# Two units' weight casts a half product earlier, one cast kept in order, and a one-column Tanh behind each Sqrt

## The chip, the cores and the metric

The kernel runs on one core of a Trainium2 chip. The metric is the device time of one execution in microseconds (us): before the change the median of three runs is 928.36 us (927.94 to 928.42). The engines are PE (matrix multiplies, with its weight loads PEld), DVE (vector), ACT (scalar: copies, casts and functions), POOL (issues stores here) and SP (issues loads here).

## The reference

One layer of a hybrid decoder, for one new sequence of 1024 tokens and for 8 single decode tokens, model width 1024. One input projection feeds an RG-LRU group and an mLSTM group of four heads:

```
hn = rmsnorm(x, g_norm);  u = hn @ w_in          # 1024 x 7176
xa, za, uq, uk, uv, uo, zb, ui, uf = split(u)
RG-LRU:  xc = causal 4-tap conv of xa
         r, i = sigmoid(block-diagonal gates of xc)      # 16 blocks of 64
         a = exp(-8 r softplus(-lambda))
         u = sqrt(-expm1(2 log a)) * (i * xc);  h_t = a_t h_(t-1) + u_t
mLSTM:   chunks of 128 tokens, running-max stabiliser, C and n carried
merged = [h * silu(za),  headnorm(sigmoid(uo) * h_mlstm) * silu(zb)]
y = rmsnorm(x + merged @ w_out, g_final)
```

The outputs are y for prompt and decode tokens and all recurrent states, in float32. The two big products, with w_in and w_out, are where most matrix work lies.

## The kernel before

**Products.** The columns of w_in are done in 14 units of 512 columns (two blocks of 256, `UNITS`, index u from 0 to 13; in tile names the unit's index is the last part of `raw_4`). A unit is a 2x2 block product done as seven products instead of eight, in the order P1, P2, P5, P6, P7, P3, P4; the number in `wh_3` is the product's place in that order, 0 to 6, so `wh_3` belongs to P6 and `wh_6` to P4. Each float32 factor is split into a rounded part and a rest, so each product needs three matmuls where one would stand: `mm3` at L64 (hi by hi), L65 and L66. In one half product that is 12 matmuls with 512 columns.

**Weight casts.** `prep` makes a product's factors: on ACT the rounded part (L278, `wh`), on DVE the rest (L281, `wl`), for some products with a sum or difference of raw blocks ahead (L272 to L275, L284). It runs two products (`LEAD = 2`) ahead of the product that uses them. `load_raw` (L217 ff.), called from `prep` of P7 and P4, issues the next unit's loads on SP. L1555 sets how far ahead: normally a product's `prep` is written ahead of the whole product; for u in 2 to 7, one that falls due with product n is written behind product n's first half.

**Evacuation.** `evac` takes each half product from PSUM: ACT copies (L321, L328, L331, L346) or DVE adds (L324, L334, L338). There are two PSUM buffers `kv`, three `o` and one each of `s`, `qp`, `tr`.

**Background work.** Between half products `pop_bg` issues one step each of queues of other work. In units 1 to 11 the main one is the RG-LRU, 16 halves (8 groups of 128 channels by 2 halves of 512 tokens) of eight steps: `conv1`, `conv2`, an empty one, `gate_a`, `gate_b`, `decay`, `scan`, `outs`. The gates are matmuls at L874 and, on ACT, a Tanh at L828 (`rg`, then `ig`; a Tanh with scaled input is the sigmoid); `gate_b`'s matmul writes the single `s` buffer that `gate_a`'s two Tanhs read. `decay` ends with a Sqrt on ACT (L896); `scan` is L900 to L902 on DVE; `outs` multiplies by the gate z (L906) and splits the result: `split` (L70 cast `rmh` on ACT, L71 rest `rml` on DVE), then two stores on POOL to `d_rm`. A decode step (`dec_unit`, L234) adds 32-row matmuls at each unit's P1 boundary, and the decode of the mLSTM adds matmuls at L1036 and ACT work at L1017.

**Order.** A scheduler orders each engine's instructions; an instruction that is pinned (`keep_in_program_order`) stays in the order written against the other pinned ones. From u = 2 on every `wh` cast is pinned. ACT holds one set of functions at a time; an `ACT_TABLE_LOAD` precedes an instruction whose function is not in the set held. Sqrt is in one set here, Tanh and Exp in another; copies and casts need no load.

Of the kernel before, what the change touches and what calls it, by code (L numbers as in the profile page):

```python
# [9 lines left out]
F32 = mybir.dt.float32  # L10
F32R = mybir.dt.float32r
BF16 = mybir.dt.bfloat16
AF = mybir.ActivationFunctionType
ALU = mybir.AluOpType
# [30 lines left out]
NWS, NSTG, LEAD = 6, 7, 2  # L45
# [4 lines left out]
def hymba_kernel(  # L50
# [7 lines left out]
    V, A, G, TE = nc.vector, nc.scalar, nc.gpsimd, nc.tensor  # L58
# [9 lines left out]
    def split(hi, lo, src):  # L68

        A.copy(hi, src)  # L70
        V.tensor_tensor(lo, src, hi.bitcast(F32), op=ALU.subtract)  # L71

    pin = tc.keep_in_program_order
# [7 lines left out]
    def ps(tag, shape):  # L81
        return psp.tile(shape, F32, tag=tag, name=f"ps_{tag}", bufs=NBUF.get(tag, 1))

    def const(shape, name, dt=F32):
        return cpool.tile(shape, dt, tag=name, name=name)
# [14 lines left out]
    def sg(shape, name, dt=F32):  # L100

        return stg.tile(shape, dt, tag="stg", name=name)
# [4 lines left out]
    def dconst(shape, name):  # L107

        return dpool.tile(shape, F32, tag=name, name=name)
# [4 lines left out]
    ones = dconst([P, P], "ones")  # L114
# [262 lines left out]
    warm = const([P, 1], "warm")  # L377
# [389 lines left out]
    def pop_bg(n=1, rg=1, dc=1):  # L767
        run_late()
        for q, m in ((bg, n), (rgq, rg), (dcq, dc)):
            for _ in range(m):  # L770
                if q:
                    q.popleft()()
# [19 lines left out]
    def rg_load(n, both=False):  # L792

        if n >= len(halves) or halves[n][0] not in rst["stored"]:
            return
        j, b = halves[n]
        if ("x", n) not in rst:
            xs = fpr["p"].tile([P, 3 + HT], F32, tag="xs", name="xs", bufs=2)
            if b == 0:
                V.memset(xs[:, 0:3], 0.0)  # L800
                ld(xs[:, 3:3 + HT], d_x[j][:, 0:HT])
            else:
                ld(xs, d_x[j][:, HT - 3:T])
            rst["x", n] = xs
        if both and ("z", n) not in rst:
            rst["z", n] = zs = fpr["p"].tile([P, HT], F32, tag="zsr", name="zsr")
            ld(zs, d_y[j][:, b * HT:(b + 1) * HT])
# [17 lines left out]
    def gate_out(rg, ig, pg, j, n):  # L825

        for m, t in enumerate((rg, ig)):
            A.activation(t[LOHI[n]], pg[LOHI[m]], AF.Tanh, scale=0.5, bias=hb[LOHI[m], j, n:n + 1])  # L828

    def rg_gw(j):  # L830
        if j < KC:
            graw = fpr["graw"][j % 2]
            for n, src in enumerate((w_rgate, w_igate)):
                for s in LOHI:
                    ld(graw[s, :, n * 64:n * 64 + 64], src[0, 2 * j:2 * j + 2].rearrange("t c d -> c t d"))

    def rg_half(j, b):
        fp = fpr["p"]
        pc = lambda r, n=1: PT[:, j, r:r + n]
        st = {}  # L840

        n = 2 * j + b

        def conv1():
            rg_load(n, True)
            xs = st["xs"] = rst["x", n]
            rg_load(n + 1)
            if b == 0:
                rg_gw(j + 1)
                ghi = fp.tile([P, 2, P], F32R, tag="ghi", name="ghi")  # L850
                glo = fp.tile([P, 2, P], F32R, tag="glo", name="glo")
                split(ghi, glo, fpr["graw"][j % 2])
                rst["g", j] = ghi, glo
            st["xc"] = xc = fp.tile([P, HT], F32, tag="xc", name="xc")
            V.tensor_scalar(xc, xs[:, 3:3 + HT], pc(R_CW + 3), pc(R_CB), op0=ALU.mult, op1=ALU.add)
            for t in (2, 1):
                V.scalar_tensor_tensor(xc, xs[:, t:t + HT], pc(R_CW + t), xc, op0=ALU.mult, op1=ALU.add)

        def conv2():
            xs, xc = st["xs"], st["xc"]  # L860
            V.scalar_tensor_tensor(xc, xs[:, 0:HT], pc(R_CW), xc, op0=ALU.mult, op1=ALU.add)
            st["xx"] = [fp.tile([P, HT], F32R, tag=t, name=t) for t in ("xh", "xl")]
            for n, s in enumerate(LOHI):
                x = st["xx"][n]
                A.copy(x[s], xc[s])
                V.tensor_tensor(x[LOHI[1 - n]], xc[s], x[s].bitcast(F32), op=ALU.subtract)
            if b == 1:
                V.tensor_copy(OC[:, j, 1:4], xs[:, HT:HT + 3])

        def gate(n):  # L870

            pg = ps("s", [P, 512])
            for k, w in enumerate(rst["g", j]):
                TE.matmul(pg, w[:, n, :], st["xx"][n], start=k == 0, stop=k == 1)  # L874
            return pg

        def gate_a():
            rg_load(n + 1)
            pg = gate(0)
            st["rg"], st["ig"] = (fp.tile([P, HT], F32, tag=t, name=m) for m, t in (("rg", "rg"), ("ig", "xh")))  # L880
            gate_out(st["rg"], st["ig"], pg, j, 0)

        def gate_b():
            pg = gate(1)
            gate_out(st["rg"], st["ig"], pg, j, 1)
            st["na"] = fp.tile([P, HT], F32, tag="xl", name="na")
            A.activation(st["na"], st["rg"], AF.Tanh, scale=sp2[:, j:j + 1], bias=sp2[:, j:j + 1])
            A.activation(st["rg"], st["rg"], AF.Exp, scale=sp4n[:, j:j + 1], bias=sp4n[:, j:j + 1])
            V.scalar_tensor_tensor(st["ig"], st["ig"], 1.0, st["xc"], op0=ALU.add, op1=ALU.mult)

        def decay():
            rg, na = st["rg"], st["na"]
            V.scalar_tensor_tensor(na, rg, 1.0, na, op0=ALU.add, op1=ALU.mult)
            V.tensor_scalar(rg, na, -1.0, 1.0, op0=ALU.mult, op1=ALU.add)
            V.scalar_tensor_tensor(na, na, 2.0, na, op0=ALU.subtract, op1=ALU.mult)
            A.activation(na, na, AF.Sqrt, scale=-0.25)  # L896

        def scan():
            rg, ig, na = st["rg"], st["ig"], st["na"]
            V.tensor_tensor(ig, ig, na, op=ALU.mult)  # L900
            V.tensor_tensor_scan(na, rg, ig, 0.0 if b == 0 else OC[:, j, 0:1], op0=ALU.mult, op1=ALU.add)
            V.tensor_copy(OC[:, j, 0:1], na[:, HT - 1:HT])  # L902

        def outs():
            na, zs = st["na"], rst["z", n]
            V.scalar_tensor_tensor(na, na, 0.5, zs, op0=ALU.mult, op1=ALU.mult)  # L906
            mh, ml = sg([P, HT], "rmh", F32R), sg([P, HT], "rml", F32R)
            split(mh, ml, na)
            stq(d_rm[0, j, :, b * HT:(b + 1) * HT], mh.bitcast(F32))
            stq(d_rm[1, j, :, b * HT:(b + 1) * HT], ml.bitcast(F32))  # L910
        return [conv1, conv2, lambda: None, gate_a, gate_b, decay, scan, outs]
# [622 lines left out]
    def preps(n):  # L1534
        for what, f in (("dec", prep_dec), ("prep", prep)):
            while what in n and state[what] < min(n[what], len(seq)):
                f(*seq[state[what]])
                state[what] += 1
# [13 lines left out]
    state["prep"] = state["dec"] = LEAD  # L1552
    part = 0
    for n, (u, q) in enumerate(seq):
        lead = {"dec": n + 1 + LEAD, "prep": n + (LEAD if u in range(2, 8) else 1 + LEAD)}  # L1555
        preps(lead)
        for _ in product(u, q):
            pop_bg(2 if u == last_u else 1, 1, part % DEC[1 if u >= DEC[0] else 2] == 1)
            preps({"prep": n + 1 + LEAD})
            part += 1  # L1560
            if u == last_u:
                wo_due((part - 1) % 14)
        if q == 6:
            for kind, j in units[u]:
                if kind == "x":
                    rg_unit(j)
            for half in range(2):
                if u == (unit_of["v", 2 * half + 1] | 1):
                    bg.append(lambda half=half: dec_rows(half))
            for h in range(NH):  # L1570
                if done_h[h] | 1 == u:
                    bg.append(lambda h=h: dcq.extend(decode_steps(h)))
            if u == last_u - 1:
                dgen = decode_outputs()

                def step():
                    next(dgen, None)
                    run_late()
                state["out"] = [step] * 5 + [m_open2]
        if not state["m"] and u > max(done_h) and not (bg or rgq or dcq or late):  # L1580
            m_start()
        if u == last_u and q == 0:
            if not state["m"]:
                while bg or rgq or dcq or late:
                    pop_bg()
                m_start()
            bg.extend(state["out"])
# [113 lines left out]
```

## Time and profile before

| what | value |
|---|---|
| median of three runs | 928.36 us |
| profiled execution, its own time | 926.71 us |
| its span, first to last instruction | 925.0 us |
| granted PE clock, mean | 0.999 |
| PE, PEld busy | 99%, 82% of the span |
| DVE, ACT, POOL busy | 77%, 62%, 17% |
| loads of a function set on ACT, by line | 16 at L896 (Sqrt), 12 at L828, the rest elsewhere |

A matmul's shown duration overlaps its neighbours': matmuls of 512 columns are shown 0.39 us long but start every 0.23 us. So PE's share of busy time says little; what counts is the time from one matmul's start to the next. In the answers shown, each row gives the start, the duration, the engine, the line, the operation, the tile written and those read, and in brackets idle time with what ended it.

### The profile page before, as it was taken

How to read it: one execution, taken by the hardware profiler on the slowest of the kernel's cores; microseconds unless marked ns; L12 is line 12 of the kernel's file. 1: busy time of each engine (PE TensorE's matmuls, PEld its weight loads, DVE VectorE, ACT ScalarE, POOL GpSimd, SP SyncE). 2: the span in 40 equal slices, each digit the busy share in tenths (PEclk: the TensorE clock that was granted, in tenths of full speed). 3: DMA queues.
4: the chain of work that ended last, by engine and by line, in shares of the span. 5: the costliest groups of instructions: out<-in, count | busy, mean ns of one | idle time of the engine just before them, and what ended most of it. 6: DMA issues, size and time to landing. Idle time of an engine off the chain costs nothing.

```text
span 925.0 us, 15327 instructions
## 1 busy us (share of the span) xinstructions
PE 912.6 (99%) x5349; PEld 760.2 (82%) x5349; DVE 708.2 (77%) x1465; ACT 574.0 (62%) x1032; POOL 154.6 (17%) x290
## 2 busy tenths in 40 slices
PE   9999999999999999999999999999999999999997
PEld 8897686878778987777789898876787888888886
DVE  6765986799788878989788866687856777667665
ACT  6753456768587767678577773447646566556552
POOL 1420111011212222222112312010201000000110
PEclk9999999999999999999999999999999999999999
DMA  7342364343656465657636553544963565465431
GB/s 242 107 133 75 116 202 160 119 160 114 207 183 237 157 217 193 208 166 251 202 128 219 181 171 129 171 145 172 346 183 121 162 186 155 115 188 155 125 84 57
DMA packets 131330, 153.69 MB, mean 166 GB/s; under 512 B 15674, under 2 KB 110018, under 8 KB 131246
## 3 DMA queue, kind: packets, MB, share of 16 engines
q1 hardware_dynamic: 113382, 96.58, 34.7%
q0 software_dynamic: 17728, 55.87, 16.5%
q8 instruction: 42, 0.69, 0.3%
q14 instruction: 34, 0.28, 0.1%
q10 hardware_dynamic: 144, 0.26, 0.1%
HBM read 101.10 MB, written 51.65 MB: 165 GB/s over the span
## 4 chain that ended last, share of the span: by engine, by line
PE 87%; DVE 5%; ACT 4%; DMA 1%; issue 1%; POOL 0%; SPq 0%; DVEq 0%; ACTq 0%; POOLq 0%
PE ps_o L64 13%; PE ps_o L66 13%; PE ps_o L65 13%; PE ps_kv L64 10%; PE ps_kv L66 10%; PE ps_kv L65 10%; PE ps_o L534 3%; PE ps_tr L234 3%; PE ps_s L1204 2%; PE ps_s L874 2%; PE ps_qp L64 1%; PE ps_tr L1345 1%; PE ps_qp L65 1%; PE ps_qp L66 1%; PE ps_qp L1036 1%
## 5 line engine op out<-in xcount | busy, mean ns | idle before, releaser
L281 DVE TENSOR_TENSOR wl<-raw,wh 128x1024 fp32r<-128x1024 f32 x91 | 111.0, 1220 | 43.0 <-ACT wh L278 28.4
L64 PE MATMUL ps_kv<-cb_hi,wh 128*128 128x512 f32 x320 | 127.1, 397 | 0.5 <-ACT s L331 0.5
L66 PE MATMUL ps_kv<-cb_hi,wl 128*128 128x512 f32 x320 | 125.3, 392 | 1.3 <-DVE wl L281 1.3
L65 PE MATMUL ps_kv<-cb_lo,wh 128*128 128x512 f32 x320 | 125.3, 392 | 0.0
L278 ACT CAST wh<-raw 128x1024 fp32r<-128x1024 f32 x91 | 95.0, 1045 | 21.2 <-DVE raw L275 6.0
L64 PE MATMUL ps_o<-cb_hi,wh 128*128 128x512 f32 x240 | 94.6, 394 | 0.0
L66 PE MATMUL ps_o<-cb_hi,wl 128*128 128x512 f32 x240 | 93.8, 391 | 0.0
L65 PE MATMUL ps_o<-cb_lo,wh 128*128 128x512 f32 x240 | 93.7, 390 | 0.0
L64 PEld LDWEIGHTS ps_kv<-cb_hi,wh 128*128 128x128 f32 x320 | 60.1, 188 | 19.3 <-issue 4.6
L66 PEld LDWEIGHTS ps_kv<-cb_hi,wl 128*128 128x128 f32 x320 | 60.1, 188 | 15.5 <-DVE wl L281 2.1
L65 PEld LDWEIGHTS ps_kv<-cb_lo,wh 128*128 128x128 f32 x320 | 60.2, 188 | 12.0
L64 PE MATMUL ps_kv<-wh,cb_hi 128*128 128x256 f32 x192 | 55.0, 287 | 0.0
L64 PEld LDWEIGHTS ps_o<-cb_hi,wh 128*128 128x128 f32 x240 | 45.1, 188 | 11.4 <-issue 2.1
L65 PE MATMUL ps_kv<-wl,cb_hi 128*128 128x256 f32 x192 | 54.4, 283 | 0.0
L66 PE MATMUL ps_kv<-wh,cb_lo 128*128 128x256 f32 x192 | 54.3, 283 | 0.0
L66 PEld LDWEIGHTS ps_o<-cb_hi,wl 128*128 128x128 f32 x240 | 45.1, 188 | 9.9 <-DVE wl L281 0.2
L64 PE MATMUL ps_o<-wo,mh 128*128 128x512 f32 (+1 forms) x136 | 53.2, 391 | 0.0
L65 PEld LDWEIGHTS ps_o<-cb_lo,wh 128*128 128x128 f32 x240 | 45.1, 188 | 9.2
L66 PE MATMUL ps_o<-wo,ml 128*128 128x512 f32 (+1 forms) x136 | 51.7, 380 | 0.0
L65 PE MATMUL ps_o<-wo,mh 128*128 128x512 f32 (+1 forms) x136 | 51.6, 380 | 0.0
L64 PE MATMUL ps_o<-wo,rh 128*128 128x512 f32 x120 | 48.3, 403 | 0.0
L66 PE MATMUL ps_o<-wo,rl 128*128 128x512 f32 x120 | 47.3, 394 | 0.0
(509 smaller groups left out, 2450.6 us busy)
## 6 DMA issues: line engine op xcount, KB each, us to landing
raw<-in_w_in_dram SPq DMA_DIRECT2D x56, 512.0 KB
Cb<-in_state_mlstm_C_dram SPq DMA_DIRECT2D x32, 256.0 KB
out_dram<-Cb POOLq DMA_DIRECT2D x32, 256.0 KB, 4.3
qk<-d_qk SPq DMA_DIRECT2D x32, 256.0 KB
oraw<-in_w_out_dram SPq DMA_DIRECT2D x16, 512.0 KB
d_qk<-s POOLq DMA_DIRECT2D x24, 256.0 KB, 3.1
x<-in_x_prompt_dram SPq DMA_DIRECT2D x8, 512.0 KB
d_x<-s POOLq DMA_DIRECT2D x16, 256.0 KB, 2.6
```

Source lines behind the costliest of these rows:

```text
L64: TE.matmul(out, ah, bh, start=first, stop=False, skip_group_check=True)
L65: TE.matmul(out, ah, bl, start=False, stop=False, skip_group_check=True)
L66: TE.matmul(out, al, bh, start=False, stop=last, skip_group_check=True)
L234: TE.matmul(dz_["p"][32 * g:32 * g + 32, :], hnd[:, k, 0:32] if second else hnd[:, k, 8:40], raws[u, k // 4][:, k % 4, :], start=k < 4 and ...
L278: o = A.copy(hi, blk(u, *src[q]))
L281: V.tensor_tensor(lo, blk(u, *src[q]), hi.bitcast(F32), op=ALU.subtract)
L534: TE.matmul(pt, op[k][x], wt, start=(k, x, y) == (0, 0, 0), stop=(k, x, y) == (7, 0, 1), skip_group_check=True)
L874: TE.matmul(pg, w[:, n, :], st["xx"][n], start=k == 0, stop=k == 1)
L1036: TE.matmul(pq[32 * g:32 * g + n, 0:256], qsel[:, kb, 4 * bb:4 * bb + n], ds_["C", h * NB + bb][:, kb, :], start=bb < 2, stop=bb >= NB - 2 ...
L1204: TE.matmul(S, qk[:, 2 + kb, :], qk[:, kb, :], start=kb == 0, stop=kb == 1)
L1345: TE.matmul(dec_o[0][32 * g:32 * g + 32, :], md, oraw[m][:, half * 512:(half + 1) * 512], start=first and m in ms[:2], stop=last and m in ...
```

## The change

Three edits. First, behind each Sqrt of the RG-LRU stands a Tanh of one column into a scratch tile (`warm`), pinned; nothing reads it. Second, in `outs` the cast of `rmh` is pinned; the subtraction is the one that `split` did. Third, L1555's range is cut from u = 2 to 7 to u = 4 to 7, so in the third and fourth units the `prep` that was behind a product's first half is ahead of the product again, with the raw loads that it issues.

```
@@ decay
             A.activation(na, na, AF.Sqrt, scale=-0.25)
+            pin(A.activation(warm, ones[:, 0:1], AF.Tanh))
@@ outs
-            split(mh, ml, na)
+            pin(A.copy(mh, na))
+            V.tensor_tensor(ml, na, mh.bitcast(F32), op=ALU.subtract)
@@ main loop
-        lead = {"dec": n + 1 + LEAD, "prep": n + (LEAD if u in range(2, 8) else 1 + LEAD)}
+        lead = {"dec": n + 1 + LEAD, "prep": n + (LEAD if u in range(4, 8) else 1 + LEAD)}
```

With the change, decay's Tanh is L897, scan L901 to L903, outs L907, the pinned cast L909 and its rest L910.

**ACT at the end of unit u = 2.** Rows in ACT's order; `wh_6` is the factor of the unit's last product, `wh_0` and `wh_1` those of the next unit, and `s` at L331 the two halves of P6. Before:

```order
L331 COPY s_1641<-ps_kv 128x512
L331 COPY s_1663<-ps_kv 128x512
L896 ACT_TABLE_LOAD
L896 ACTIVATE na<-na 128x512
L278 CAST wh_5_1647<-raw_2_1290 128x1024
L865 CAST xh<-xc 64x512
L70 CAST rmh<-na 128x512
L278 CAST wh_6_1689<-raw_2_1290 128x1024
L865 CAST xl<-xc 64x512
L278 CAST wh_0_1741<-raw_3_1602 128x1024
L346 COPY c_1771<-ps_kv 128x512
L828 ACT_TABLE_LOAD
```

With the change:

```order
L278 CAST wh_5_1629<-raw_2_1290 128x1024
L331 COPY s_1645<-ps_kv 128x512
L331 COPY s_1664<-ps_kv 128x512
L278 CAST wh_6_1669<-raw_2_1290 128x1024
L896 ACT_TABLE_LOAD
L896 ACTIVATE na<-na 128x512
L897 ACT_TABLE_LOAD
L897 ACTIVATE warm<-ones 128x1
L865 CAST xh<-xc 64x512
L909 CAST rmh<-na 128x512
L278 CAST wh_0_1720<-raw_3_1580 128x1024
L865 CAST xl<-xc 64x512
```

`wh_5` and `wh_6` now stand ahead of the Sqrt instead of behind it, and the load for Tanh follows the Sqrt instead of standing ahead of the gate.

**PE at the boundary of units u = 2 and 3.** The last matmul of P4, the decode matmuls (L234) and the gate's (L874). Before:

```order
L66 MATMUL ps_kv<-cb_hi_169,wl_6_1690 128x512
L234 MATMUL ps_tr<-raw_3_1602,hnd 32x512
L874 MATMUL ps_s<-xl,ghi 128x512
L874 MATMUL ps_s<-xl,glo 128x512
L234 MATMUL ps_tr<-raw_3_1602,hnd 32x512 x3
L234 MATMUL ps_tr<-raw_3_1693,hnd 32x512 x4
```

With the change:

```order
L66 MATMUL ps_kv<-cb_hi_169,wl_6_1670 128x512
L874 MATMUL ps_s<-xl,ghi 128x512
L874 MATMUL ps_s<-xl,glo 128x512
L234 MATMUL ps_tr<-raw_3_1580,hnd 32x512 x4
L234 MATMUL ps_tr<-raw_3_1673,hnd 32x512 x4
```

The gate's pair no longer stands inside the decode group.

**DVE in unit u = 4, around P6.** `wl_3` is the rest of P6's factor; L901 (before) or L902 (with the change) that writes `na` from `rg` and `ig` is the scan. Before:

```order
L900 TENSOR_TENSOR ig<-ig,na 128x512
L861 SCALAR_TENSOR_TENSOR xc<-xs,PT,xc 128x512
L281 TENSOR_TENSOR wl_3_2267<-raw_4_1958,wh_3_2266 128x1024
L901 SCALAR_TENSOR_TENSOR na<-rg,OC,ig 128x512
L800 MEMSET xs 128x3
L923 COPY dxs<-dxc 64x8
L902 COPY OC<-na 128x1
L906 SCALAR_TENSOR_TENSOR na<-na,zsr 128x512
```

With the change:

```order
L901 TENSOR_TENSOR ig<-ig,na 128x512
L861 SCALAR_TENSOR_TENSOR xc<-xs,PT,xc 128x512
L902 SCALAR_TENSOR_TENSOR na<-rg,OC,ig 128x512
L800 MEMSET xs 128x3
L925 COPY dxs<-dxc 64x8
L903 COPY OC<-na 128x1
L907 SCALAR_TENSOR_TENSOR na<-na,zsr 128x512
L281 TENSOR_TENSOR wl_3_2271<-raw_4_1938,wh_3_2270 128x1024
```

`wl_3` moves behind the scan, two small copies and L907. On ACT the cast `wh_3` that it needs stands right behind the Sqrt before, and behind Sqrt, load and one-column Tanh with the change.

## The prediction

> **What bounds the kernel now.** I read the page first, then the waits of PE from 100 to 600 us, where the projection and the RG-LRU run, then PE's timeline at each gap, then ACT and DVE there. The page:
>
> ```profile
> PE 912.6 (99%) x5349; PEld 760.2 (82%) x5349; DVE 708.2 (77%) x1465; ACT 574.0 (62%) x1032; POOL 154.6 (17%) x290
> ```
>
> PE sets the end. The edits add no matmul, so they can only take gaps between matmuls away or make new ones. The waits view (engine, line waited at, releaser: us, times, longest) names how much there is to take:
>
> ```profile
> PE ps_kv L66 <- DVE wl L281: 1.3, 2, 1.0
> PE ps_s L874 <- ACT ig L828: 0.7, 2, 0.5
> PE ps_kv L64 <- ACT s L331: 0.5, 1, 0.5
> ```
>
> This understates it, since a matmul's shown duration runs into the next one's. I measure from start to start, and take off the 0.23 us at which 512-column matmuls normally follow:
>
> ```profile
> 149.97 0.39 PE L65 MATMUL ps_kv<-cb_lo,wh 128*128 128x512 f32 x1
> 150.68 0.50 PE L66 MATMUL ps_kv<-cb_hi,wl 128*128 128x512 f32 x1 [0.32 <-DVE wl L281]
> ...
> 194.91 0.40 PE L65 MATMUL ps_kv<-cb_lo,wh 128*128 128x512 f32 x1
> 196.26 0.50 PE L66 MATMUL ps_kv<-cb_hi,wl 128*128 128x512 f32 x1 [0.96 <-DVE wl L281]
> 196.60 0.40 PE L64 MATMUL ps_kv<-cb_hi,wh 128*128 128x512 f32 x1
> ...
> 261.62 0.39 PE L64 MATMUL ps_o<-cb_hi,wh 128*128 128x512 f32 x1
> 262.49 0.50 PE L874 MATMUL ps_s<-xl,ghi 128*128 128x512 f32 x1 [0.48 <-ACT ig L828]
> ...
> 313.38 0.28 PE L66 MATMUL ps_kv<-wh,cb_lo 128*128 128x256 f32 x1
> 313.72 0.50 PE L874 MATMUL ps_s<-xl,ghi 128*128 128x512 f32 x1
> ...
> 409.29 0.39 PE L64 MATMUL ps_o<-cb_hi,wh 128*128 128x512 f32 x1
> 410.18 0.50 PE L64 MATMUL ps_kv<-cb_hi,wh 128*128 128x512 f32 x1 [0.50 <-ACT s L331]
> ...
> 418.52 0.39 PE L66 MATMUL ps_o<-cb_hi,wl 128*128 128x512 f32 x1
> 419.16 0.50 PE L874 MATMUL ps_s<-xl,ghi 128*128 128x512 f32 x1 [0.25 <-ACT ig L828]
> ```
>
> So the gaps are 0.48, 1.12, 0.64, 0.22 (0.34 less the 0.12 of a 256-column matmul), 0.66 and 0.41 us. After a wait the next start follows 0.34 us later (196.26 to 196.60) instead of 0.23, so each wait costs 0.11 more. All six together are 4.2 us, 0.45% of the time. Nothing that the edits touch can give much more, except one thing that the waits view does not show, a decode group cut in two at the end of u = 2; beside it a whole one:
>
> ```profile
> 156.39 1.04 PE L234 MATMUL ps_tr<-raw,hnd 128*32 128x512 f32 x2
> 157.37 0.50 PE L874 MATMUL ps_s<-xl,ghi 128*128 128x512 f32 x1
> ...
> 159.88 0.50 PE L64 MATMUL ps_kv<-cb_hi,wh 128*128 128x512 f32 x1
> ...
> 426.54 1.92 PE L234 MATMUL ps_tr<-raw,hnd 128*32 128x512 f32 x16
> 428.40 0.50 PE L64 MATMUL ps_kv<-cb_hi,wh 128*128 128x512 f32 x1
> ```
>
> Cut, the stretch takes 159.88 - 156.39 = 3.49 us with the gate's pair in it. Whole, the group takes 1.86; the pair in a run of full matmuls is 2 x 0.23 = 0.46.
>
> **The change, part by part.** *Earlier casts in u = 2 and 3 (gain).* ACT at the end of u = 2:
>
> ```profile
> 140.89 0.63 ACT L896 ACTIVATE na<-na 128x512 f32<-128x512 f32 x1
> ...
> 148.31 1.05 ACT L278 CAST wh<-raw 128x1024 fp32r<-128x1024 f32 x1
> ...
> 153.89 1.28 ACT L828 ACT_TABLE_LOAD   x1
> 155.19 0.68 ACT L828 ACTIVATE rg<-ps_s,hb 64x512 f32<-64x512 f32 x1
> ```
>
> The cast at 148.31 is `wh_6`; its rest makes PE wait at 149.97. In the new order it stands ahead of the Sqrt, some 8 us earlier, so the rest is done long before, and the wait goes: 0.48 + 0.11 = 0.59. The raw loads move ahead on SP with `prep`, so the next unit's casts get their data no later; their queue holds only RG-LRU loads that are not used for several us. With the load for Tanh gone from 153.89, `rg` and `ig` are done about 1.3 us earlier, and the pair at L874 stands ahead of the decode group: 3.49 becomes 1.86 + 0.46 = 2.32, a gain of 1.17. Its bounds: 0, if the cut was not what made the group slow, and 1.2. I take 1.17, since the whole group's row is the same work. In u = 3 DVE shows why PE waits at 194.91:
>
> ```profile
> 193.87 1.22 DVE L901 TENSOR_TENSOR_SCAN na<-rg,ig 128x512 f32<-128x512 f32 x1
> 195.01 1.20 DVE L281 TENSOR_TENSOR wl<-raw,wh 128x1024 fp32r<-128x1024 f32 x1
> ```
>
> `wl_6` is queued behind the scan, since its cast was behind the Sqrt. With the cast a half product (12 x 0.23 = 2.7 us) earlier and ahead of the Sqrt, 1.12 + 0.11 = 1.23 go. Together 2.99.
>
> *The one-column Tanh.* The page's groups show 16 loads for the Sqrts; the loads back stand today ahead of the next Tanh, and now stand behind the Sqrt. Their number is unchanged. Added are 16 one-column Tanhs; the nearest row is the same tile at the start:
>
> ```profile
> L378 ACT ACTIVATE warm<-ones x1: 203/203/203, 2.0 to 2.0; 128x1 f32<-128x1 f32 x1
> ```
>
> So 16 x 0.20 = 3.2 us more on ACT, busy 62%: free wherever ACT idles afterwards. What moves matters more: 1.28 + 0.20 = 1.48 us now stand between each Sqrt and whatever ACT has next. Where that was a gate, PE's wait goes. At 262.49 the load was at 259.76 in front of `rg` and `ig`; 1.28 earlier, `ig` is done at about 261.2, before the pair's turn (261.85): gain 0.64 + 0.11 = 0.75. At 313.72, the same: 0.22 + 0.11 = 0.33.
>
> Where what follows the Sqrt is a weight cast, it is late. In u = 4 (P6):
>
> ```profile
> 216.63 0.63 ACT L896 ACTIVATE na<-na 128x512 f32<-128x512 f32 x1 [1.78 <-DVE na L895]
> ...
> 219.90 1.21 DVE L281 TENSOR_TENSOR wl<-raw,wh 128x1024 fp32r<-128x1024 f32 x1
> 221.03 1.27 DVE L901 TENSOR_TENSOR_SCAN na<-rg,OC,ig 128x512 f32<-128x512 f32 x1
> ...
> 222.75 0.69 DVE L906 SCALAR_TENSOR_TENSOR na<-na,zsr 128x512 f32<-128x512 f32 x1
> ...
> 221.83 0.39 PE L66 MATMUL ps_kv<-cb_hi,wl 128*128 128x512 f32 x1
> ```
>
> The Sqrt ends at 217.26; 1.48 later `wh_3` starts, 218.8, and ends at 219.8. That alone would be in time. But DVE's new order runs the scan and L906 first: scan from 219.90, L906 from about 221.6, `wl_3` from 222.2 to 223.4. PE needs it at 221.83; its new order puts one more L64 and L65 of P6 ahead, 0.45, so 222.28. The wait is 1.1 and its restart 0.11: a loss of 1.2. Queued behind that L66 is every later matmul. Bounds: 0, if the scheduler's order lets the rest come at the old 221.1, and 1.7 without the two matmuls. In u = 7 (P6) the same pieces stand closer:
>
> ```profile
> 352.22 0.63 ACT L896 ACTIVATE na<-na 128x512 f32<-128x512 f32 x1 [2.45 <-DVE na L895]
> ...
> 355.42 1.20 DVE L281 TENSOR_TENSOR wl<-raw,wh 128x1024 fp32r<-128x1024 f32 x1
> ...
> 357.00 0.50 PE L66 MATMUL ps_kv<-cb_hi,wl 128*128 128x512 f32 x1
> ```
>
> `wh_3` ends at 352.85 + 1.48 + 1.04 = 355.4; on DVE, where only the scan stood ahead, a copy, L906 and another copy now go first too, 0.9 us more, so `wl_3` runs from 356.4 to 357.6, and PE comes to it at 357.0: a loss of 0.6 + 0.11 = 0.7. Bounds 0 and 1.3.
>
> In u = 5 (P7) ACT's copy behind the Sqrt moves too:
>
> ```profile
> 272.51 0.56 ACT L331 COPY s<-ps_kv 128x512 f32<-128x512 f32 x1
> ```
>
> It becomes 1.48 later, done near 274.1. PE has three `o` matmuls more in front of the `kv` buffer that it frees (0.7 us); I count 0.1, bounds 0 and 0.4. Small reorderings of L1036 and the decode transposes around u = 7/8: 0.1, bounds -0.2 and 0.3.
>
> *The pinned cast.* `rmh` sits behind a wait for DVE, with `wh` casts and copies behind it on ACT. At 410.18 PE waits for a copy that stands behind `rmh`; in the new order the copies and matmuls pass each other so that this wait mostly goes (0.66 + 0.11). But the next wait, at 419.16, hangs on another chain:
>
> ```profile
> 415.63 0.63 ACT L352 ACTIVATE tz<-s 128x512 f32<-128x512 f32 x1 [1.36 <-DMA d_rm<-rmh]
> ```
>
> That Tanh waits for `rmh`'s store to land, and `rg` and `ig` of the gate are behind it. The store is issued no sooner, so what PE wins at 410 it waits longer at 419: I count 0 for u = 8, bounds -0.3 and +0.8. From u = 9 on the rests are ready 3 us and more ahead, and the edits cost nothing there: the matmuls of the earlier products cover them.
>
> Sum: gains 2.99 + 0.75 + 0.33 = 4.07; losses 1.2 + 0.7 + 0.1 + 0.1 = 2.1; net 2.0 us. The profiled execution takes 926.71 (span 925.0 and 1.7 around it) and becomes 924.7. The median of the runs is 1.65 above the profiled one, so I add that: **926.4 us**, 0.2% faster.
>
> **The rivals.** *New waits do not come.* If DVE and ACT run `wl_3` in time in u = 4 and 7, only the gains are left: 928.36 - 4.07 + 0.2 = 924.5, and up to 0.8 less if u = 8 keeps its part, 923.7. For it: before, `wl_3` had 0.7 and 0.4 us to spare. Against: the listed order is what the engines run, and 1.48 is more than either.
>
> *The waits trade places.* The decode group was slow for another reason (its 1.17 is not gained) and the u = 4 and 7 waits are as summed: 4.07 - 1.17 - 2.1 = 0.8, 927.6, no change. For it: such a group has one clean example beside it, not a test.
>
> *Load and Tanh on the path (slower).* One mechanism: 1.48 us between a Sqrt and the ACT work that PE needs next, in u = 4, 5, 7 and 8. With nothing to spare at these four places each costs 1.48 + 0.11 = 1.6, 6.4 in all, against 4.07: 2.3 slower, 930.7. It decides from the point where the four exceed 5.9 (a loss of 0.2%). For it: u = 4 and 7 have under 1 us in hand. Against: in u = 5 and 8 PE has other matmuls in front.
>
> *A switch of sets costs more than its row.* If the load back held ACT as long again as its row (1.28 more), `wh_3` of u = 7 would end at 356.7, `wl_3` 0.3 later than summed, and the copy in u = 5 would be done at 275.4 instead of 274.1, 1.3 of it seen by PE: 1.6 less gain, 928.0, no change. Against: the load at 153.89 ends at 155.17 and `rg` starts at 155.19; nothing stands between. 0.02. The Trainium skill (ScalarE: Activation LUTs, What ACT_TABLE_LOAD costs) is the page for it: it counts about 1380 ns of drain beside 1283 ns of load in every switch. The load's figure agrees with the row's 1.28 us, the drain does not appear in this trace, and the row decides.
>
> *The change doesn't do what it says.* The Tanh could have been ordered elsewhere than behind its Sqrt; in the order all 16 follow directly, so I leave 0.01, with the time before.
>
> **How the numbers follow.** A measurement of this kernel tells 0.2% (1.86 us) from no change, so faster is below 926.5 and slower above 930.2. My forecast (net gain 1 to 3 us: 925.4 to 927.4) has 0.42, no new waits 0.21, waits that trade places 0.18, load and Tanh on the path 0.16, a dearer switch 0.02, no effect 0.01. Faster: half of the first (0.21) and all of the second (0.21), 0.42; slower: 0.11 of the path rival, whose milder third stays within 0.2%; same: the remaining 0.47. Range 924.2 to 929.6: below it lies part of the no-new-waits case (0.07), above it most of the path rival's slower part (0.1).
>
> **What would show it.** Right: no gap at the P4 of u = 2 and 3, L874 ahead of an uncut L234 group in u = 2 (2.3 us), no load ahead of `rg` in u = 5 and 6; and new PE waits for `wl` at P6 of u = 4 (about 1.1) and u = 7 (0.6), with DVE's L281 behind L907 there. In u = 8 a longer wait at the gate and none at L331. Wrong: waits of 1.5 us for L331 copies in u = 5 or 8 (slower), no wait at P6 (faster), or an L234 group that is still 3 us when whole.

## The result: 0.76% slower, and the profile after

The changed kernel takes 934.87 us (median of five runs, 934.51 to 937.36) where the kernel before takes 928.36. The quotient of these two medians is 1.0070; the ratio that was measured, and that the text goes by, is 1.0076 (95% interval 1.0064 to 1.0088). The forecast was 926.4 us, faster; the measured time is slower and lies outside the forecast's range. The page of the profiled execution (934.87 us, span 933.1), its busy line, and the waits of PE from 100 to 620 us (line waited at, releaser: us, times, longest):

```profile
PE 916.2 (98%) x5349; PEld 762.7 (82%) x5349; DVE 708.9 (76%) x1465; ACT 575.2 (62%) x1048; POOL 154.7 (17%) x290
```

```profile
PE ps_tr L234 <- DMA raw<-in_w_in_dram: 2.6, 3, 1.6
PE ps_o L64 <- DVE s L324: 2.4, 1, 2.4
PE ps_kv L66 <- DVE wl L281: 1.8, 2, 1.2
PE ps_s L874 <- ACT ig L828: 0.5, 1, 0.5
```

The engines do the same work as before; PE stands still in other places. Two of the four rows name releasers that are absent from that view of before: a raw load, and a DVE evacuation (L324). To place them, the two traces are lined up below: the same matmul of the same unit, its start after less its start before.

| start before, us | place | after less before | since the row above | forecast for it |
|---|---|---|---|---|
| 165.0 | u = 3, P1 (past P4 and the gate of u = 2) | -1.8 | -1.8 | -1.8 |
| 215.0 | u = 4 (past P4 of u = 3) | -3.2 | -1.4 | -1.2 |
| 240.1 | past P6 of u = 4 | -1.7 | +1.5 | +1.2 |
| 266.0 | past the gate of u = 5 | -2.5 | -0.7 | -0.75 |
| 300.0 | start of u = 6 | -1.9 | +0.5 | +0.1 |
| 320.0 | past the gate of u = 6 | -2.1 | -0.2 | -0.33 |
| 330.1 | end of u = 6 | -2.0 | +0.2 | 0 |
| 345.0 | u = 7, P1 | -0.1 | **+1.8** | 0 |
| 372.0 | past P6 of u = 7 | +0.8 | +0.9 | +0.7 |
| 395.0 | u = 8, P1 | +1.6 | +0.8 | +0.1 |
| 416.0 | u = 8, P7 to P4 | +0.9 | -0.6 | 0 |
| 425.0 | past the gate of u = 8 | +1.2 | +0.2 | 0, with the row above |
| 451.9 | u = 9 | +5.3 | **+4.1** | 0 |
| 490.1 | u = 10 | +6.1 | **+0.8** | 0 |
| 560.0 | u = 11 | +7.2 | +1.1 | 0 |
| 700.0 | mLSTM part | +8.3 | +1.1 | 0 |

Up to 320 us the forecast holds place by place, but for 0.4 us between 266 and 300. From there on PE loses 10.4 us, where the forecast has 0.8.

**What came as forecast.** PE at the boundary of u = 2 and 3, after (it answers the rows at 156.39 to 159.88 of before):

```profile
155.71 0.39 PE L874 MATMUL ps_s<-xl,ghi 128*128 128x512 f32 x1
155.94 0.40 PE L874 MATMUL ps_s<-xl,glo 128*128 128x512 f32 x1
156.26 1.92 PE L234 MATMUL ps_tr<-raw,hnd 128*32 128x512 f32 x16
158.12 0.50 PE L64 MATMUL ps_kv<-cb_hi,wh 128*128 128x512 f32 x1
```

The pair of the gate stands in a run of full matmuls, the decode group is whole, and the stretch takes 158.12 - 155.71 = 2.41 us where it took 3.49. In u = 4, DVE and PE after:

```profile
216.83 1.27 DVE L902 TENSOR_TENSOR_SCAN na<-rg,OC,ig 128x512 f32<-128x512 f32 x1
...
218.55 0.69 DVE L907 SCALAR_TENSOR_TENSOR na<-na,zsr 128x512 f32<-128x512 f32 x1
219.16 1.22 DVE L281 TENSOR_TENSOR wl<-raw,wh 128x1024 fp32r<-128x1024 f32 x1
...
220.43 0.50 PE L66 MATMUL ps_kv<-cb_hi,wl 128*128 128x512 f32 x1 [1.21 <-DVE wl L281]
...
357.80 0.50 PE L66 MATMUL ps_kv<-cb_hi,wl 128*128 128x512 f32 x1 [0.64 <-DVE wl L281]
```

`wl_3` comes behind the scan and L907 and PE waits 1.2 us; in u = 7 (last row) 0.6.

**What was not forecast, 1: the raw load of u = 7.** SP, DVE and PE around the boundary of u = 6 and 7, before and then after:

```profile
326.53 1.20 DVE L281 TENSOR_TENSOR wl<-raw,wh 128x1024 fp32r<-128x1024 f32 x1
327.76 0.94 SPq L217 DMA_DIRECT2D raw<-in_w_in_dram  x2
329.02 0.34 SPq L807 DMA_DIRECT2D zsr<-d_y  x1
334.99 1.93 PE L234 MATMUL ps_tr<-raw,hnd 128*32 128x512 f32 x16
```

```profile
325.53 0.37 SPq L807 DMA_DIRECT2D zsr<-d_y  x1
325.94 1.22 DVE L281 TENSOR_TENSOR wl<-raw,wh 128x1024 fp32r<-128x1024 f32 x1
327.18 0.94 SPq L217 DMA_DIRECT2D raw<-in_w_in_dram  x2
333.04 1.07 PE L234 MATMUL ps_tr<-raw,hnd 128*32 128x512 f32 x8
335.69 1.06 PE L234 MATMUL ps_tr<-raw,hnd 128*32 128x512 f32 x8 [1.59 <-DMA raw<-in_w_in_dram]
```

The last rest of u = 6 (`wl_6`, the L281 row) is the last reader of a raw block; when it ends (325.94 + 1.22), the load of u = 7's block is issued. PE is 2 us earlier than before, and this load only 0.6 us, because `wl_6` now stands on DVE behind L903, L907 and L338, and the load of zsr has gone first. The decode group needs the whole block: its second half waits.

**2: DVE in u = 9.** DVE and PE after:

```profile
427.33 0.17 DVE L868 COPY OC<-xs 128x3 f32<-128x3 f32 x1 [3.11 <-DMA xs<-d_x]
...
445.68 1.27 DVE L324 TENSOR_TENSOR s<-s,ps_o 128x512 f32<-128x512 f32 x2
...
443.63 0.39 PE L66 MATMUL ps_o<-cb_hi,wl 128*128 128x512 f32 x1
446.42 0.79 PE L64 MATMUL ps_o<-cb_hi,wh 128*128 128x512 f32 x1 [2.40 <-DVE s L324]
447.01 0.63 PE L65 MATMUL ps_o<-cb_lo,wh 128*128 128x512 f32 x1
447.44 0.63 PE L66 MATMUL ps_o<-cb_hi,wl 128*128 128x512 f32 x1
...
449.57 0.46 PE L65 MATMUL ps_o<-cb_lo,wh 128*128 128x512 f32 x1
```

A copy of three columns (L868, part of `conv2` of the half two behind the one at hand) was ordered ahead of work that was ready, and held DVE for 3.11 us until its xs had landed. DVE was busy without a gap from there on, and 18 us later an evacuation was late for PE. Before, the copy stands behind the scan of the half at hand, and waits for nothing:

```profile
434.26 0.16 DVE L868 COPY OC<-xs 128x3 f32<-128x3 f32 x1
...
441.86 1.28 DVE L324 TENSOR_TENSOR s<-s,ps_o 128x512 f32<-128x512 f32 x2
```

After the 2.4 us the matmuls start every 0.43 us instead of 0.23 until 449.6. The windows view (PE, PEld, DVE, ACT, POOL busy, then the granted clock, DMA share, GB/s) gives the clock there:

```profile
446.00:448.00 2.00, 1.58 (x4) 1.30 (x5) 1.94 (x4) 0.59 (x2) 1.11 (x2) 0.57 0.62 216
448.00:450.00 2.00, 2.00 (x7) 1.57 (x6) 1.97 (x4) 0.00 (x0) 0.13 (x1) 0.58 0.63 227
```

So the wait cost 446.42 - 443.63 - 0.23 = 2.56 us start to start, and some 1.6 us more at a reduced clock: about 4.1 together, as in the table.

**3: the raw load of u = 10.** On SP the load stands behind a zsr load, and the decode group is cut in the same way as in u = 7. Before, then after:

```profile
461.68 0.99 SPq L217 DMA_DIRECT2D raw<-in_w_in_dram  x2
464.91 0.34 SPq L807 DMA_DIRECT2D zsr<-d_y  x1
470.45 1.92 PE L234 MATMUL ps_tr<-raw,hnd 128*32 128x512 f32 x16
```

```profile
467.83 0.34 SPq L807 DMA_DIRECT2D zsr<-d_y  x1
468.96 0.94 SPq L217 DMA_DIRECT2D raw<-in_w_in_dram  x2
475.76 1.06 PE L234 MATMUL ps_tr<-raw,hnd 128*32 128x512 f32 x8
477.59 1.07 PE L234 MATMUL ps_tr<-raw,hnd 128*32 128x512 f32 x8 [0.76 <-DMA raw<-in_w_in_dram]
```

The load is also issued later against PE: 6.8 us ahead of the group's first matmul, where it was 8.8 us before.

### The profile page after: what moved, and what is told of

It is laid out like the page before. It is cut to its first block, busy times and chain, and to the rows that moved or that the text cites. A ratio compares the mean times of both kernels' runs of the same rounds, so it can differ in the third digit from the quotient of the medians.

```text
span 933.1 us, 15358 instructions
## 1 busy us (share of the span) xinstructions
PE 916.2 (98%) x5349; PEld 762.7 (82%) x5349; DVE 708.9 (76%) x1465; ACT 575.2 (62%) x1048; POOL 154.7 (17%) x290
## 4 chain that ended last, share of the span: by engine, by line
PE 75%; DVE 10%; DMA 6%; issue 4%; ACT 3%; POOL 1%; SPq 0%; DVEq 0%; POOLq 0%; ACTq 0%
PE ps_o L64 12%; PE ps_o L66 11%; PE ps_o L65 11%; PE ps_kv L64 8%; PE ps_kv L66 8%; PE ps_kv L65 8%; DMA raw<-in_w_in_dram 3%; PE ps_o L534 3%; PE ps_tr L234 2%; DVE wl L281 2%; PE ps_s L1206 2%; PE ps_s L874 1%; DMA xs<-d_x 1%; PE ps_qp L64 1%; DVE na L902 1%
## 5 line engine op out<-in xcount | busy, mean ns | idle before, releaser
L281 DVE TENSOR_TENSOR wl<-raw,wh 128x1024 fp32r<-128x1024 f32 x91 | 111.1, 1221 | 40.9 <-ACT wh L278 26.6
```

The source lines that it names most:

```text
L281: V.tensor_tensor(lo, blk(u, *src[q]), hi.bitcast(F32), op=ALU.subtract)
```

## The experiments

The kernel before was timed beside every experiment and its median lay between 926.89 and 928.36, so the ratios to it are what is compared.

The pinned cast does nothing. Two of the kernels below lack it: the one without the eighth Tanh has the whole change's order of instructions on every engine outside 320 to 336 us, and the one with the Tanhs of n = 0 to 8 has it up to 376 us. (n counts the halves from 0; the n-th Tanh stands behind the n-th half's Sqrt.) So the kernels below leave the pinned cast out, except the three that pin a copy or a zsr load.

**Each edit alone.** The range of the late casts:

```
-... (LEAD if u in range(2, 8) else 1 + LEAD)}
+... (LEAD if u in range(4, 8) else 1 + LEAD)}
```

> Only the range of the late casts is cut (u = 4 to 7), no Tanh and no pinned cast. Theory A (each edit acts at its own place; the harm is the Tanh's): the two waits for wl_6 in u = 2 and 3 go, 0.59 + 1.23 = 1.8 us, and the decode group in u = 2 stays cut since the load in front of the gate is still there: 926.5. Rival B (the raw loads, now issued earlier, collide with other transfers, and that is the harm): 930 or more, with waits for raw at L234.

Measured: 924.55 us, ratio 0.9965 (0.9953 to 0.9978), 3.3 us faster. Its trace has no wait for `wl` in u = 2 and 3 and a decode group in u = 2 that is still cut; PE is 1.9 us earlier than before from u = 4 on, as expected. The measured gain is nearer 3 than the 1.8 expected, though the interval reaches down to 2.0; the profiled execution (926.40) is the slowest of the six, so its trace does not tell why. Rival B falls: the time is shorter, not longer, and the one wait for raw at L234 in the trace is 0.26 us, at u = 7.

The Tanh:

```
+            pin(A.activation(warm, ones[:, 0:1], AF.Tanh))
```

> Only the one-column Tanh behind each Sqrt. Theory A: all of the harm, and without the gain at wl_6: 934.87 + 1.8 = 936.7 or somewhat more (936 to 938), with the same waits at 330 to 480 us as with the whole change. Rival B (the harm needs the earlier casts): under 930.

Measured: 942.41 us, ratio 1.0157 (1.0129 to 1.0185). This is more than the 936 to 938 expected: all of the harm, and twice as much as the whole change shows, so the edits do not add. The waits from u = 7 to 10 that theory A expected are there (1.45 us for raw at u = 7, 2.22 for L324 at u = 9, 0.50 for raw at u = 10). In u = 3 the late casts meet the Tanh, and it goes on to the raw load of u = 4:

```profile
195.59 0.50 PE L64 MATMUL ps_kv<-cb_hi,wh 128*128 128x512 f32 x1 [1.27 <-ACT wh L278]
197.66 0.50 PE L66 MATMUL ps_kv<-cb_hi,wl 128*128 128x512 f32 x1 [0.88 <-DVE wl L281]
206.29 1.57 PE L234 MATMUL ps_tr<-raw,hnd 128*32 128x512 f32 x8 [2.81 <-DMA raw<-in_w_in_dram]
```

With casts a half product late, the Tanh costs there what the range edit takes away: at 204 us of before this kernel is 5.9 us behind, the whole change 3.2 ahead, 9 us of difference.

**The copy that held DVE.**

```
             if b == 1:
-                V.tensor_copy(OC[:, j, 1:4], xs[:, HT:HT + 3])
+                pin(V.tensor_copy(OC[:, j, 1:4], xs[:, HT:HT + 3]))
```

> The whole change, and the copy of 3 columns at L868 pinned behind the last vector instruction written before it, so that it stands in conv2 of its own half; nothing else moves on any engine. Theory A (DVE stood still 3.11 us at this copy, which waited for the load of xs two halves ahead of its use, and this made PE wait 2.4 us at 446 and then run at a granted clock of 0.57 for 3.4 us): 934.87 - 2.56 - 1.6 = 930.7, and no clock below 0.9 from 444 to 452. Rival B (DVE is behind there anyway, the copy only takes the blame): 934 to 935.

Measured: 931.94 us, ratio 1.0045 (1.0028 to 1.0061), 2.9 us less than the whole change. The edit moves more than was expected: the line runs for eight halves, all eight copies are pinned, and on SP some loads of xs and zsr change places with them. In its trace the waits for L324 are gone and the clock stays up:

```profile
446.00:448.00 2.00, 2.00 (x11) 1.65 (x10) 1.94 (x4) 0.60 (x2) 1.11 (x2) 1.00 0.60 223
```

Against the trace of the whole change it wins 4.1 us between 372 and 450, as forecast; but in this execution the wait for raw at u = 7 was 3.07 us instead of 1.59, with a reduced clock behind it, which hides part of it. Theory A holds: DVE's idle time at the copy was the cause, not a general backlog. That the other moved rows are not the cause is borne out by the two kernels with split Tanhs below, where no copy is pinned: the wait for L324 is missing where the copy stands behind the scan, and there where it stands ahead.

**The raw loads.** First the order on SP alone:

```
-            ld(zs, d_y[j][:, b * HT:(b + 1) * HT])
+            pin(ld(zs, d_y[j][:, b * HT:(b + 1) * HT]))
```

> The whole change, and the loads of zsr pinned on SP behind the load written before them; only SP's order changes. With it the second raw load of u = 10 stands ahead of the zsr load again, in u = 7 it still stands behind. Theory A (a raw load queued behind a zsr load that waits for the product with the old zsr is what PE waits for at 476): 1.35 us less there, 933.5, the wait at 333 unchanged. Rival B (the raw load is late because its buffer is freed late): no change, 934.9.

Measured: 934.28 us, ratio 1.0076 (1.0059 to 1.0093): no difference to be measured in the time. In the trace the decode group of u = 10 is whole and waits for nothing:

```profile
470.01 0.92 SPq L217 DMA_DIRECT2D raw<-in_w_in_dram  x2
470.98 0.63 SPq L807 DMA_DIRECT2D zsr<-d_y  x1
476.74 1.92 PE L234 MATMUL ps_tr<-raw,hnd 128*32 128x512 f32 x16
```

From the issue of the load to the group's second half it takes 8.6 us with the whole change and at most 7.6 here, where the second half waits for nothing. So zsr ahead of raw was worth about 1 us at u = 10. The load itself is issued no sooner against PE than with the whole change (6.7 us ahead of the group), since here, too, `wl_6` frees the block. At u = 7, where zsr still goes first, this execution waited 2.82 us.

Second, the whole change without the eighth Tanh (ahead of P4 of u = 6):

```
+            if n in (0, 1, 2, 3, 4, 5, 6, 8, 9, 10, 11, 12, 13, 14, 15):
+                pin(A.activation(warm, ones[:, 0:1], AF.Tanh))
```

> The whole change without the one-column Tanh behind the Sqrt of the eighth half only (n = 7, in u = 6 ahead of P4). No matmul moves; on SP the second raw load of u = 7 stands ahead of the zsr load again. Theory A (PE waits at 333 for that raw load because a zsr load of 256 KB went first while the DMA engines were full): the wait for raw at the decode group of u = 7 falls from 2.2 to about 0.4 us, 1.8 us less in all, ratio to the whole change 0.998. Rival B (the raw load is late because its buffer is freed late by wl_6 of u = 6, which stays behind the scan here): the wait stays at 1.5 us or more.

Measured: 932.35 us, ratio 1.0052 (1.0038 to 1.0066), about 2.2 us less than the whole change, and the wait at u = 7 is gone:

```profile
324.23 1.20 DVE L281 TENSOR_TENSOR wl<-raw,wh 128x1024 fp32r<-128x1024 f32 x1
325.46 0.94 SPq L217 DMA_DIRECT2D raw<-in_w_in_dram  x2
326.71 0.34 SPq L807 DMA_DIRECT2D zsr<-d_y  x1
332.67 1.93 PE L234 MATMUL ps_tr<-raw,hnd 128*32 128x512 f32 x16
```

The expectation had one thing wrong: `wl_6` did not stay where it was. Without the Tanh it is still behind the scan, but ahead of the three rows that stood between (the copy, L338 and the product with z); it ends 1.7 us sooner, and the load is issued 0.03 us after its end. So both suspects moved at once.

Third, zsr alone:

```
@@ rg_load
-            ld(zs, d_y[j][:, b * HT:(b + 1) * HT])
+            o = ld(zs, d_y[j][:, b * HT:(b + 1) * HT])
+            if n == 8:
+                pin(o)
@@ conv1
-            rg_load(n, True)
+            rg_load(n, n != 8)
@@ gate_a
+            if n == 8:
+                rg_load(n, True)
```

> The whole change, and the zsr load of the ninth half (n = 8) written in gate_a instead of conv1 and pinned, so that on SP it stands behind the second raw load of u = 7; no other row moves on any engine. wl_6 of u = 6 stays behind the scan. Theory A (the raw load is late because 256 KB of zsr go first): the wait for raw at the decode group of u = 7, 1.6 to 3.1 us in four traces of this order, falls under 0.8, ratio 1.0052 as without the eighth Tanh. Rival B (the raw load is issued late because its buffer is freed only when wl_6 is done, at 327.2 instead of 325.5): the raw load is issued at 327 again, the wait stays above 1.5 and the ratio above 1.006.

Measured: 933.18 us, ratio 1.0063 (1.0049 to 1.0077), between the two:

```profile
325.54 1.22 DVE L281 TENSOR_TENSOR wl<-raw,wh 128x1024 fp32r<-128x1024 f32 x1
326.79 0.99 SPq L217 DMA_DIRECT2D raw<-in_w_in_dram  x2
334.92 1.06 PE L234 MATMUL ps_tr<-raw,hnd 128*32 128x512 f32 x8 [1.22 <-DMA raw<-in_w_in_dram]
```

The load is issued when `wl_6` ends, as rival B has it, and PE still waits 1.2 us; with zsr ahead it waited 1.6 to 3.1 us in five traces. Both parts count: the late release, and the transfer in front. The intervals of the times can't tell how much is each one's, but the traces give a size. From the issue of the load to the group's second half it takes 8.1 us here, and 8.5, 9.7, 9.8, 10.0 and 10.1 in the five traces with zsr ahead. With the range alone, where zsr is behind as well, it takes 8.5. So the late release leaves 1.2 us of wait, and zsr in front adds up to 0.4 us in the trace of the whole change and 1.3 to 1.9 in the other four.

**The cast of P6 in u = 4.** The whole change without the fourth Tanh (the edit of the kernel without the eighth, with 3 left out of the list instead of 7):

> The whole change without the one-column Tanh behind the Sqrt of the fourth half only (n = 3, in u = 4 ahead of P6). On DVE wl_3 stands where it stood before, ahead of the scan. Theory A: the wait for wl_3 at P6 of u = 4 (1.2 us with its restart) goes, and PE is 1.2 us earlier from there to 330; behind that, part is eaten by the wait for raw at 333: 0 to 1.2 us less in all. Rival B (the wait only moves to the next product of u = 4): nothing gained at 250 already.

Measured: 932.54 us, ratio 1.0041 (1.0025 to 1.0056). Against the trace of the whole change PE is 1.2 us earlier from 221 on, as theory A has it, and the gain is not only moved to the next product. The time gains more than expected (0 to 1.2 us): by the ratios 3.2 us. The profiled execution was the slowest of its runs (937.57, with 3.13 us of wait for raw at u = 7), so its trace does not tell why.

**Late and early places apart.** If the harm is a sum of places, the Tanhs can be split:

```
+            if n < 9:                               # the one kernel
+            if n in (0, 4, 6, 9, 10, 11, 12, 13, 14, 15):   # the other
+                pin(A.activation(warm, ones[:, 0:1], AF.Tanh))
```

> Late casts for u = 4 to 7, the one-column Tanh behind the Sqrts of n = 0 to 8 only. At u = 4, 6 and 7 the orders are those of the whole change; the copy L868 of u = 9 stands behind the scan again, as before, and the raw load of u = 10 ahead of zsr. Theory A (the harm is the sum of separate places): the waits at 220, 333 and 357 as with the whole change, none at 446 and 476: 934.9 - 4.2 - 1.0 = 929.7, ratio 1.002. Rival B (the late places only suffer because PE and DVE come late from u = 7): 446 and 476 keep their waits, 933 or more.

> Late casts for u = 4 to 7, the Tanh behind the Sqrts of n = 0, 4, 6 and 9 to 15. At u = 4, 6 and 7 the orders are those of before; L868 of u = 9 stands ahead of L889 and the xs load, as with the whole change, and the second raw load of u = 10 behind zsr. Theory A: no wait at P6 of u = 4 and 7 and none for raw at u = 7, but the waits at u = 9 and u = 10: 922.4 + 4.2 + 1.0 = 927.6, ratio 1.000. Rival B: the waits at u = 9 and 10 do not come when u = 7 is in time, and it stays at 922 to 923.5.

Measured: 930.06 us, ratio 1.0020 (1.0007 to 1.0032), and 927.79 us, ratio 1.0002 (0.9990 to 1.0013). Both as theory A has them. The first has no wait at u = 9 and 10, although PE comes to u = 9 two us later than with the whole change. In the second, PE is in time at u = 4 and 7, and u = 9 fails all the same; its DVE, then PE:

```profile
421.50 0.17 DVE L868 COPY OC<-xs 128x3 f32<-128x3 f32 x1 [2.54 <-DMA xs<-d_x]
...
440.59 0.50 PE L64 MATMUL ps_o<-cb_hi,wh 128*128 128x512 f32 x1 [1.84 <-DVE s L324]
```

**The Tanh only where a gate comes next.**

```
+            if n in (0, 4, 6):
+                pin(A.activation(warm, ones[:, 0:1], AF.Tanh))
```

> The late casts for u = 4 to 7 only, and the one-column Tanh behind three Sqrts only: n = 0 (u = 2), 4 and 6, where a gate and no weight cast comes next on ACT. SP's order at u = 7 and 10 is the one of before, and so is DVE's at u = 4, 6 and 7. Theory A: the gain of the range alone (3.3 us) and on top the whole decode group in u = 2 (1.2) and the two gates in u = 5 and 6 (0.75 and 0.33), 2.2 more: 922.3 where before takes 927.9, ratio 0.994. Rival B (what is won by u = 6 is waited for at the raw load of u = 7): as the range alone, 924.5, ratio 0.9965.

Measured: 922.45 us (921.88 to 923.75), ratio 0.9943 (0.9930 to 0.9955), 5.3 us faster than before. PE's waits from 100 to 700 us are one row:

```profile
PE ps_kv L64 <- ACT s L331: 0.5, 1, 0.5
```

It is faster than both kernels. On top of the range alone the three Tanhs bring 2.1 us, as theory A has it (2.2); the two intervals just touch, but the traces agree: PE is 4.3 us earlier than before at 330 us, and 1.9 us with the range alone.

## Why the prediction was wrong

- **"Earlier casts in u = 2 and 3", 2.99 us: right.** 3.2 in the trace. The decode group, which the waits view doesn't show, gave what the whole group's row promised.
- **The gates of u = 5 and 6, 0.75 and 0.33: right** (0.7 and 0.2). So is the sign named for u = 8: no wait at L331, a longer one at the gate (0.48 us at 420). Of the 0.6 us won at L331 the gate took back only 0.2; the forecast had 0 for both, with bounds that hold it.
- **The rests of P6, 1.2 and 0.7: right** (1.2 and 0.6 of wait, 1.5 and 0.9 start to start). Rival "new waits do not come" is out.
- **"From u = 9 on the rests are ready 3 us and more ahead, and the edits cost nothing there": wrong.** This is the step that failed most. The rests are ready, but other rows of DVE moved too: L868 came to stand ahead of ready work, and while it waited for its load all of DVE stood still. Cost: 4.1 us, of which 1.6 is the clock.
- **The raw loads of later units: put at nothing without a reason.** "The raw loads move ahead on SP with prep, so the next unit's casts get their data no later" was said of u = 2 and 3, and holds there. The sum has no term for the raw loads of u = 7 and 10. There SP has zsr ahead of raw, and at u = 7 the rest `wl_6` of u = 6, in time for its own product, is late in freeing the block for the next unit's load. Cost: 1.8 and 0.8 us.
- **"Small reorderings ... around u = 7/8: 0.1": too small**, 0.8. It comes with the Tanhs from n = 9 on: in the trace with those of n = 0 to 8 it is missing, in that with n = 0, 4, 6 and 9 to 15 it is 0.4. The 1.1 us of u = 11 come with them too: the second trace has them, the first has not. PE's weight loads wait there for `Cb`, at 520 us.
- **The rest.** Of the 0.5 us between 266 and 300, 0.45 lies at the decode group of u = 6, whose second half waits 0.26 us for its raw load, the third of the three raw waits in the view. The 1.1 us at 660 to 670, with a wait of 0.18 for a load of w_out, stays open: kernels without late Tanhs show 0.3 to 1.0 there too.
- **A small slip.** The copy of u = 5 would by its row end at 272.51 + 0.56 + 1.48 = 274.55, not near 274.1. It changed nothing: PE lost nothing there, where 0.1 was forecast.
- **The rival on the slower side** had the right culprit, the Tanh, and the wrong mechanism. The 1.48 us on ACT never stood on PE's path at the L331 copies (u = 5 and 8). The Tanh worked through the order it gave DVE and SP. *The dearer switch* is out as well: in the whole change the load behind the Sqrt takes 1.28 us and the Tanh starts 0.01 us later.
- The chance of 0.11 for slower was too low: its one mechanism was priced at u = 4, 5, 7 and 8 alone, and none of the costs at u = 9 and 10 nor the raw load of u = 7 had a rival.

## What to carry to other kernels

When an edit makes a scheduler reorder an in-order engine, walk its order to the end and ask of each moved instruction not only who waits for its result but what it frees and what it waits for itself: a three-column copy with a DMA wait in front of ready work stopped DVE for 3.1 us, and a rest that was in time for its product was late for the load that needed its buffer. Compare the DMA queue's order too. An edit that is good behind three of sixteen instructions may be bad behind the rest; take it where the next instruction on the engine profits.

## What the hardware showed

In these traces a PE idle time of little over 2 us is followed by half the clock. The 0.43 us steps follow idle times of 2.20, 2.22, 2.40, 2.44 and 2.45 us on the L324 wait in five traces (some six to nine matmuls, beginning up to five matmuls after the restart) and 2.8 to 3.1 us on raw loads in five; after 2.04 and 1.84 us on the same L324 wait in two other traces, and after 1.6 us and less, the steps stay 0.23. (The idle time is the one that the view gives in brackets; 2.20 is 2.59 from start to start.) In the whole change the two windows above show 2 x 0.43 + 2 x 0.42 = 1.7 us of clock not granted, and 1.6 us were lost on top of the wait. Whether the length alone decides between 2.04 and 2.20 us is not shown. The Trainium skill (TensorE: Matmul & The Clock Gate, Part 1: The HAM clock gate) has the clock fall to half after an idle window of about 3.4 us; the half rate agrees with the 0.43 against 0.23, the length does not: here 2.2 us are enough.

The wait for one load also differs between traces with zsr ahead of it and PE within 0.2 us up to that load: for raw at u = 7, 1.6 us in the trace of the whole change, 2.8 and 3.1 us in those with the pinned zsr loads and the pinned copy. In the trace with the pinned zsr loads the orders up to there are those of the whole change but for one zsr load on SP, at 219 to 228 us.
